# Near attention in a one-core encoder block: scaling the probabilities, or scaling the output

## The chip, the cores and the metric

The kernel runs on one core of one Trainium2 chip. The metric is the device time of one execution in microseconds, as the median of several executions. A profile is of one execution; its times are counted from the start of its span, and it names the engines PE (TensorE, the matmul engine, with PEld for its weight loads), DVE (VectorE), ACT (ScalarE), POOL (GpSimd) and SP (SyncE, which issues most transfers).

## What is computed

One layer of a bidirectional encoder on 1024 tokens of width 1024, in float32: layer norm, one combined projection, dilated attention in three groups of heads, a gated linear recurrence in both directions (HGRN2), gated merge, and a SwiGLU feed-forward part. The change lies in the attention, where each group of heads gives its own softmax output and the three are mixed with weights that come from their softmax denominators:

```python
def dilated_attention(aq, ak, av, slopes):
    ...
    for g, (window, dil) in enumerate(ATT_GROUPS):
        o, lse = dilated_group(aq[:, :, g], ak[:, :, g], av[:, :, g], window, dil, slopes[g])
        outs.append(o)
        lses.append(lse)
    w = jax.nn.softmax(jnp.stack(lses), axis=0)
    o = jnp.sum(w[..., None] * jnp.stack(outs), axis=0)
    return o.reshape(b, s, ATT_WIDTH).astype(aq.dtype)
```

Group 0 has a window of 128 tokens without dilation: this is the near attention. Groups 1 and 2, with dilations 4 and 16, are the far attention. For each token and head the kernel needs the exponentials of the near scores, their sum, and one factor that puts near and far on the same maximum and divides by the common sum.

## The kernel before, in words

All of the work runs in three phases. Phase 1, which holds the change, has a main stream and side units that are woven into it.

The stream (`stream`, lines 467 to 548) is the combined projection, in tiles of 128 columns. Four tiles at a time are computed by a seven-product scheme (`ORDER`); each product is four blocks of three matmuls (`mm3`, lines 253 to 257), because each operand is split into a rounded part and a rest. These matmuls write PSUM banks called `pj`, two for each group `g`. A product's weights are split by ScalarE (`w_hi`, line 205) and GpSimd (`w_lo`, line 209) three products ahead; sums of weight blocks are made at lines 488 to 493; a finished product is evacuated by VectorE or ScalarE (lines 401 to 430, and 511) before its bank can be written again.

Side units run in this order for each of four pairs of heads `j`: an HGRN head, another, the far attention (`att_far`), the near attention (`att_near`). Each unit is a generator. After each of its pieces it yields a number, which is how many products of the stream are issued before its next piece (`phase1`, lines 1124 to 1155). Within this, a scheduler at build time orders the instructions of each engine by its own estimate of their times, so an edit also shifts instructions around it. Each engine then runs its queue strictly in order. All side units share four PSUM banks (`ps_sd`) and nine SBUF slots of 128x1024 (`slot`), which are reused from unit to unit.

The near attention of one pair of heads (lines 780 to 892), as before:

- Scores: matmuls at line 811 for eight tiles of 128 queries and two heads; VectorE adds the bias and takes the row maximum (line 595); ScalarE takes the exponential with the row sum (line 827). Queries lie on the partitions, keys along the row. The exponentials lie in `P`, in slots 3, 4, 5 and 8.
- V is turned by TensorE (line 587) and copied by ScalarE (line 588).
- Factors (lines 833 to 842): `NM` is the common maximum, `W0` and `W12` become the factors of near and far for each query, 128x16 values each.
- Spread: GpSimd copies `W12`, each value 64 times, into `RB` (line 845, slot 1).
- Scaling: VectorE multiplies each row of each tile of `P` by `W0` (line 849): 18 instructions, fourteen of 128x256 and four of 64x128.
- Turn: TensorE transposes `P` tile by tile (line 863), VectorE and ScalarE copy the result back into `P` (lines 612 and 610).
- `RB` is transposed (line 870) into two banks `RL`, so that the factor of each query stands along the row.
- Output: matmuls of V and the turned `P` (line 883) into two banks `O`.
- Join: `OL`, the far output in slot 7, is multiplied by `RL` (line 888), `O` is added (line 890), and `OL` is stored (line 891).

Three of the four near units are followed by an HGRN head. It fetches into slots 1, 0 and 3, writes `qd` into slot 2 and, into slot 7, `fb` (line 937). Its scans and reciprocals are on VectorE (lines 953, 964, 967), its keys are finished by GpSimd (lines 961 and 965) and transposed by TensorE (line 982).

Of the kernel before, what the change touches and what calls it, by code (L numbers as in the profile page):

```python
# [14 lines left out]
OP = mybir.AluOpType  # L15
# [7 lines left out]
HALF = 512  # L23
# [56 lines left out]
class Block:  # L80
# [699 lines left out]
    def att_near(self, j, pre):  # L780


        nc, ident, HD, d = self.nc, self.ident, self.HD, self.at_d[j]
        OL, N12, L12 = self.far
# [6 lines left out]
        def rows(tt, hd):  # L791

            w = P[tt // 2][:, hd, tt % 2, :]
            if tt:
                return ((slice(0, 128), w),)
            return (slice(64, 128), w[64:128, 128:256]), (slice(0, 64), w[0:64, 0:128])
# [36 lines left out]
        NM, W0, W12 = (self.att_small(n) for n in ("NM", "W0", "W12"))  # L833
# [7 lines left out]
        for w in (W0, W12):  # L841
            nc.vector.tensor_mul(w, w, L0)

        RB = self.slot(1, "rb", (8, 2, 64))
        nc.gpsimd.tensor_copy(RB, W12.rearrange("p a t -> p t a")[:, :, :, None].to_broadcast([128, 8, 2, 64]))
        for tt in range(8):
            for hd in range(2):
                for p, z in rows(tt, hd):
                    nc.vector.tensor_scalar(z, z, W0[p, hd, tt:tt + 1], None, op0=OP.mult)  # L849
        yield 2  # L850

        kw = dict(skip_group_check=True)
# [4 lines left out]
        for b in range(4):  # L857
            for hd in range(2):
                ps = self.ps_sd()
# [4 lines left out]
                self.copied(hd, P[b][:, hd].rearrange("p t c -> p (t c)"), ps)  # L864
            if b % 2:
                yield b
        RL = [self.ps_sd(), self.ps_sd()]
        for tt in range(8):
            c = 128 * (tt % 4)
            nc.tensor.transpose(RL[tt // 4][:, c:c + 128], RB[:, tt].rearrange("p a d -> p (a d)"), ident)  # L870
        O = [self.ps_sd(), self.ps_sd()]
        todo = []
        for kt in range(8):
            c = 128 * (kt % 4)

            todo.append((kt, O[kt // 4], c + (64 if kt == 0 else 0), c + 128, kt, 192 if kt == 0 else 128))
            t = kt + 1
# [9 lines left out]
        for b, src, dst in cols:  # L887
            nc.vector.tensor_mul(OL[:, dst], OL[:, dst], RL[b][:, src])
        for b, src, dst in cols:
            nc.vector.tensor_add(OL[:, dst], OL[:, dst], O[b][:, src])  # L890
        nc.scalar.dma_start(self.att_d[j], OL)
        yield -1

# [843 lines left out]
```

## Time and profile before

| what | value |
|---|---|
| three executions | 2123.66, 2134.19, 2137.27 us; median 2134.19 |
| the profiled execution | 2131.49 us, its span 2129.7 us |
| mean granted clock of TensorE | 0.987 of full speed |
| near attention, pair 0 to 3: scaling from about | 360, 616, 868 and 1133 us |
| line 849: instructions, shortest, median, longest | 72: 278, 340 and 1268 ns |
| lines 888 and 890: instructions, median | 12 each: 617 and 610 ns |
| TensorE waits for line 849 | 8.6 us in 8 waits |

A row of the timeline has the start, the length, engine, line, operation, result<-operands, shapes and a count; what stands in brackets is the idle time of the engine before it and what ended that. Matmuls are pipelined, so the length of one is longer than the distance to the next. A row of the stretches has the length, the busy time of each engine (with its instructions), the granted clock, the share of the transfer engines and their GB/s. In a row of waits stand the waiting engine and line, what it waited for, the total in us, how often, and the longest.

### The profile page before, as it was taken

Reading aid. Unit: us, or ns where it says so; the run is one execution under the profiler, and the core shown is the slowest. Engines: PE = TensorE matmul, PEld = TensorE weight load, DVE = VectorE, ACT = ScalarE, POOL = GpSimd, SP = SyncE. Lnnn points to the kernel's source line nnn. Section 1 sums busy time; section 2 is a strip of 40 time slices with the busy share of each in tenths; the row PEclk is TensorE's granted clock in tenths of the full one; section 3 lists DMA queues with packets and bytes.
Section 4 is the critical chain, followed back from the end, with each engine's and each line's share of the span. In section 5 each row is a group of like instructions: output and inputs, shape, how many; then the busy total and the mean of one; then the engine's idle time right before and its main releaser. Section 6 shows DMA issues by size and latency. Waiting matters only on the chain.

```text
span 2129.7 us, 30900 instructions
## 1 busy us (share of the span) xinstructions
PE 2029.0 (95%) x10941; PEld 1674.6 (79%) x10941; DVE 1392.7 (65%) x2228; ACT 919.7 (43%) x1864; POOL 1077.5 (51%) x882
## 2 busy tenths in 40 slices
PE   4799999999999999999999899999999999999998
PEld 3678787788878788887888688878788888887876
DVE  7667746777459753788536712337867677767778
ACT  6544455434544435543355432135433333343542
POOL 3466653567536664465644754443656566630012
PEclk9899999999999999999999999999999999999999
DMA  5342442435424343333444755244434344348423
GB/s 202 109 133 95 147 155 73 144 118 167 130 92 141 135 146 125 124 129 109 146 130 142 283 188 164 89 139 139 154 109 153 129 144 134 117 160 291 158 89 124
DMA packets 273885, 301.10 MB, mean 141 GB/s; under 512 B 14081, under 2 KB 205378, under 8 KB 273730
## 3 DMA queue, kind: packets, MB, share of 16 engines
q1 hardware_dynamic: 266272, 273.73, 39.7%
q10 hardware_dynamic: 7458, 25.40, 3.0%
q8 instruction: 86, 1.41, 0.3%
q14 instruction: 69, 0.57, 0.1%
HBM read 200.25 MB, written 98.83 MB: 140 GB/s over the span
## 4 chain that ended last, share of the span: by engine, by line
PE 77%; DVE 12%; issue 5%; POOL 3%; DMA 2%; ACT 2%; SPq 0%; ACTq 0%; DVEq 0%; POOLq 0%
PE pj L255 17%; PE pj L256 17%; PE pj L257 16%; PE sd L256 6%; PE sd L255 6%; PE sd L257 6%; PE sd L1049 2%; POOL w_lo L209 1%; DVE qd L964 1%; DVE qd L967 1%; PE sd L998 1%; DVE p L849 1%; PE sd L863 1%; DVE fb L953 1%; ACT p L827 1%
## 5 line engine op out<-in xcount | busy, mean ns | idle before, releaser
L209 POOL TENSOR_TENSOR w_lo<-wa,w_hi 128x512 fp32r<-128x512 f32 x276 | 377.4, 1374 | 297.9 <-ACT w_hi L205 274.0
L205 ACT CAST w_hi<-wa 128x512 fp32r<-128x512 f32 x276 | 170.4, 619 | 245.8 <-PE pj L256 159.5
L209 POOL TENSOR_TENSOR w_lo<-wsum,w_hi 128x512 fp32r<-128x512 f32 x88 | 129.0, 1474 | 113.0 <-PE sd L257 60.4
L200 POOL TENSOR_TENSOR mv<-mv,mhalf 128x1 f32<-128x1 f32 x24 | 15.5, 647 | 228.6 <-DVE mv L199 225.5
L209 POOL TENSOR_TENSOR w_lo<-f_raw,w_hi 128x512 fp32r<-128x512 f32 x66 | 102.1, 1555 | 55.4 <-ACT w_hi L205 54.2
L255 PE MATMUL pj<-xt1hi,w_hi 128*128 128x512 f32 x260 | 103.9, 400 | 16.3 <-ACT xt1hi L205 10.7
L205 ACT CAST w_hi<-wsum 128x512 fp32r<-128x512 f32 x88 | 54.7, 621 | 124.6 <-PE sd L256 114.4
L255 PE MATMUL pj<-xb22hi,w_hi 128*128 128x512 f32 x260 | 102.6, 394 | 1.1 <-ACT wkeep L511 1.1
L256 PE MATMUL pj<-xt1lo,w_hi 128*128 128x512 f32 x260 | 102.3, 393 | 0.0
L257 PE MATMUL pj<-xt1hi,w_lo 128*128 128x512 f32 x260 | 102.0, 392 | 0.0
L256 PE MATMUL pj<-xb22lo,w_hi 128*128 128x512 f32 x260 | 101.5, 390 | 0.0
L257 PE MATMUL pj<-xb22hi,w_lo 128*128 128x512 f32 x260 | 101.3, 390 | 0.0
L209 POOL TENSOR_TENSOR w_lo<-ws,w_hi 128x512 fp32r<-128x512 f32 x46 | 63.0, 1373 | 69.2 <-ACT w_hi L205 63.3
L205 ACT CAST gwsum<-a_raw 128x512 fp32r<-128x512 f32 (+1 forms) x78 | 47.8, 616 | 102.9 <-PE pj L256 48.0
L511 ACT COPY wkeep<-pj 128x512 f32<-128x512 f32 x138 | 80.1, 582 | 22.1 <-DVE evh L430 10.1
L403 DVE TENSOR_TENSOR evh<-wkeep,pj 128x512 f32<-128x512 f32 x66 | 57.5, 879 | 48.5 <-PE pj L257 35.2
L209 DVE TENSOR_TENSOR gwkeep<-a_raw,gwsum 128x512 fp32r<-128x512 f32 (+1 forms) x78 | 57.7, 739 | 43.1 <-ACT gwsum L205 40.2
L489 POOL TENSOR_TENSOR wa<-wa,wa 128x512 f32<-128x512 f32 x46 | 67.6, 1480 | 35.6 <-DVE ws L488 27.6
L414 DVE TENSOR_TENSOR evh<-wkeep,pj 128x512 f32<-128x512 f32 x48 | 32.6, 681 | 80.7 <-PE pj L257 65.5
L255 PE MATMUL pj<-xt4hi,w_hi 128*128 128x512 f32 x192 | 77.8, 406 | 5.6 <-DVE evh L403 5.6
L257 PE MATMUL pj<-xt2hi,w_lo 128*128 128x512 f32 x192 | 76.1, 397 | 4.9 <-POOL w_lo L209 4.9
L255 PE MATMUL pj<-xb11hi,w_hi 128*128 128x512 f32 x192 | 77.3, 404 | 2.6 <-DVE evh L414 1.4
(406 smaller groups left out, 6587.1 us busy)
## 6 DMA issues: line engine op xcount, KB each, us to landing
wa<-in_w_in_dram SPq DMA_DIRECT2D x184, 256.0 KB, 3.1
f_raw<-in_w_ffn_in_dram SPq DMA_DIRECT2D x44, 512.0 KB, 4.2
a_raw<-gd SPq DMA_DIRECT2D x30, 512.0 KB, 3.5
gd<-fc SPq DMA_DIRECT2D x44, 256.0 KB, 2.0
gd<-fs SPq DMA_DIRECT2D x33, 256.0 KB, 2.1
tg<-evh SPq DMA_DIRECT2D x32, 256.0 KB, 3.5
tg<-tg SPq DMA_DIRECT2D x16, 512.0 KB, 3.7
y<-ahs SPq DMA_DIRECT2D x16, 512.0 KB, 5.5
```

Source lines behind the costliest of these rows:

```text
L205: nc.scalar.copy(hi, src)
L209: ins = e.tensor_sub(lo, src, hi.bitcast(F32))
L255: nc.tensor.matmul(ps, whi, xhi, start=first, stop=False, **kw)
L256: nc.tensor.matmul(ps, whi, xlo, start=False, stop=False, **kw)
L257: nc.tensor.matmul(ps, wlo, xhi, start=False, stop=last, **kw)
L403: self.left(nc.vector.tensor_tensor(o, self.order_src(add, g, kind), s, OP.add))
L414: self.left(nc.vector.tensor_add(t, add, ps))
L489: nc.gpsimd.tensor_sub(a["a21"], a["a11"], a["a21"])
L511: nc.scalar.copy(t, ps)
L827: nc.scalar.activation(z, z, AF.Exp, bias=N0[p, hd, tt:tt + 1], scale=QSCALE, accum_out=L0[p, hd, tt:tt + 1])
L849: nc.vector.tensor_scalar(z, z, W0[p, hd, tt:tt + 1], None, op0=OP.mult)
L1049: nc.tensor.matmul(po[:, jj, :], l, r, start=(n == 0), stop=(n == len(terms) - 1))
```

## The change

The probabilities are transposed as the exponentials leave them, without the factor. `W0` is spread by GpSimd into a second tile in the same way as `W12`, in slot 2, which held the keys of the near attention. That tile is transposed ahead of the other by eight more matmuls, and ScalarE copies the result into an SBUF tile `near`, also in slot 2. After the output matmuls, `near` is multiplied by the near output, and the product is added to the scaled far output. The 18 multiplications of line 849 are gone; in their place stand three of the shape of line 888. In the built order, the output matmuls stand 18 stream matmuls behind the spread's transposes, where before they followed them directly.

```diff
-        RB = self.slot(1, "rb", (8, 2, 64))
-        nc.gpsimd.tensor_copy(RB, W12.rearrange("p a t -> p t a")[:, :, :, None].to_broadcast([128, 8, 2, 64]))
-        for tt in range(8):
-            for hd in range(2):
-                for p, z in rows(tt, hd):
-                    nc.vector.tensor_scalar(z, z, W0[p, hd, tt:tt + 1], None, op0=OP.mult)
+        RB = [self.slot(1 + i, f"rb{i}", (8, 2, 64)) for i in range(2)]
+        for r, w in zip(RB, (W12, W0)):
+            nc.gpsimd.tensor_copy(r, w.rearrange("p a t -> p t a")[:, :, :, None].to_broadcast([128, 8, 2, 64]))
         yield 2
...
-        RL = [self.ps_sd(), self.ps_sd()]
-        for tt in range(8):
-            c = 128 * (tt % 4)
-            nc.tensor.transpose(RL[tt // 4][:, c:c + 128], RB[:, tt].rearrange("p a d -> p (a d)"), ident)
+        def spread(r):
+            out = [self.ps_sd(), self.ps_sd()]
+            for tt in range(8):
+                c = 128 * (tt % 4)
+                nc.tensor.transpose(out[tt // 4][:, c:c + 128], r[:, tt].rearrange("p a d -> p (a d)"), ident)
+            return out
+
+        near = self.slot(2, "near")
+        for b, ps in enumerate(spread(RB[1])):
+            nc.scalar.copy(near[:, HALF * b:HALF * (b + 1)], ps)
+        RL = spread(RB[0])
         O = [self.ps_sd(), self.ps_sd()]
...
         for b, src, dst in cols:
-            nc.vector.tensor_add(OL[:, dst], OL[:, dst], O[b][:, src])
+            z = slice(HALF * b + src.start, HALF * b + src.stop)
+            nc.vector.tensor_mul(near[:, z], near[:, z], O[b][:, src])
+            nc.vector.tensor_add(OL[:, dst], OL[:, dst], near[:, z])
         nc.scalar.dma_start(self.att_d[j], OL)
```

## The prediction

> **What bounds the kernel now.** I read the page first (shares of the span), then the chain that ended last, then who TensorE waits for, and last the four near-attention stages themselves, stretch by stretch and instruction by instruction.
>
> ```profile
> span 2129.7 us, 30900 instructions
> PE 2029.0 (95%) x10941; PEld 1674.6 (79%) x10941; DVE 1392.7 (65%) x2228; ACT 919.7 (43%) x1864; POOL 1077.5 (51%) x882
> PE   4799999999999999999999899999999999999998
> PEclk9899999999999999999999999999999999999999
> PE 77%; DVE 12%; issue 5%; POOL 3%; DMA 2%; ACT 2%; SPq 0%; ACTq 0%; DVEq 0%; POOLq 0%
> ```
>
> TensorE is busy for 2029.0 of 2129.7 us. An edit is worth what it does to TensorE: idle time taken away, matmuls added, or time at a lower granted clock. The other engines count only where TensorE waits for them. Of its 100 us of idle time, this is what the near attention owns (view of TensorE's waits):
>
> ```profile
> PE sd L863 <- DVE p L849: 8.6, 8, 2.0
> PE pj L255 <- DVE evh L403: 9.3, 4, 3.4
> ```
>
> The first line is the target: eight waits, two in each of the four near stages, in which the transposes of the probabilities (L863) stand behind VectorE's scaling (L849). The stage of head pair 0:
>
> ```profile
> 352.58 1.03 PE L587 MATMUL sd<-tabs_sb,v 128*128 128x128 f32 x8
> 357.10 0.39 PE L256 MATMUL pj<-xb21lo,w_hi 128*128 128x512 f32 x1
> 358.17 1.05 ACT L588 COPY v<-sd 128x512 f32<-128x512 f32 x2
> 359.82 0.39 PE L256 MATMUL pj<-xb21lo,w_hi 128*128 128x512 f32 x1
> 360.32 7.56 DVE L849 TENSOR_SCALAR p<-p,W 64x128 f32<-64x128 f32 x18
> 360.36 1.04 POOL L845 COPY rb<-W 128x1024 f32<-128x1024 f32 x1 [0.98 <-DVE W L842]
> 361.35 1.26 POOL L209 TENSOR_TENSOR w_lo<-wa,w_hi 128x512 fp32r<-128x512 f32 x1
> 362.75 0.65 PE L863 MATMUL sd<-tabs_sb,p 128*128 128x128 f32 x2 [1.86 <-DVE p L849]
> 364.26 3.30 PE L863 MATMUL sd<-tabs_sb,p 128*128 128x128 f32 x14 [0.87 <-DVE p L849]
> ```
>
> The stream's matmuls follow each other every 0.227 us (12 of them, 357.10 to 359.82). VectorE gets the factor W0 only at 360.3 and needs 7.56 us for 18 multiplications; TensorE stops twice, for 1.86 and 0.87 us. The four stages by stretch (us, then busy time of TensorE, its weight load, VectorE, ScalarE, GpSimd, then granted clock, DMA share, GB/s):
>
> ```profile
> 360.00:370.00 10.00, 7.27 (x27) 5.76 (x27) 9.88 (x24) 2.23 (x6) 3.48 (x3) 0.66 0.00 1
> 616.00:624.00 8.00, 6.09 (x33) 4.39 (x32) 7.94 (x19) 1.60 (x4) 3.19 (x3) 1.00 0.09 33
> 868.00:878.00 10.00, 7.99 (x36) 6.56 (x36) 9.84 (x23) 3.16 (x7) 3.13 (x3) 0.83 0.19 54
> 1134.00:1142.00 8.00, 6.01 (x34) 4.85 (x34) 7.95 (x19) 1.34 (x3) 3.61 (x3) 1.00 0.33 96
> ```
>
> Idle: 2.73 + 1.91 + 2.01 + 1.99 = 8.6 us, the sum of the waits above. In the first and third stage the granted clock falls as well: 7.27 busy us x (1 - 0.66) = 2.5 and 7.99 x (1 - 0.83) = 1.4, together 3.9 us of slow running.
>
> **The change, part by part.**
>
> *Removed: 72 scalings on VectorE (18 a stage).* The first transposes now need only the exponentials of row tiles 0 to 3 and PSUM. In the order of instructions as built, they stand 24 stream matmuls behind the transposes of V (L587) in every stage, where before there were 24 to 32. In stage 0, V's transposes end at about 353.4, so TensorE comes at 353.4 + 24 x 0.227 = 358.8. Of the four "sd" banks two are free by then and two wait for ScalarE's copies of V, which end at 358.7 and 359.2; the eight transposes ahead of that need take 0.9 us. So the wait goes: 8.6 us, and with it, if the dip is the stall's doing, 3.9 us of clock. What is late next is nothing on TensorE's own queue: the row factors are needed only 38 to 48 stream matmuls later (9 to 11 us), for the spread's transposes.
>
> *Added on TensorE: 8 more transposes a stage, 32 in all.* The same operation, by its line (minimum, median, maximum ns) and sixteen in one run:
>
> ```profile
> L863 PE MATMUL sd<-tabs_sb,p x128: 270/273/475, 362.7 to 1145.1; 128*128 128x128 f32 x128
> 878.40 1.91 PE L863 MATMUL sd<-tabs_sb,p 128*128 128x128 f32 x16
> 379.99 1.35 DVE L888 TENSOR_TENSOR ol<-ol,sd 128x448 f32<-128x448 f32 x3 [3.96 <-PE sd L870]
> 385.79 1.32 DVE L890 TENSOR_TENSOR ol<-ol,sd 128x512 f32<-128x512 f32 x3
> 377.18 0.58 ACT L511 COPY wkeep<-pj 128x512 f32<-128x512 f32 x1
> ```
>
> (1.91 - 0.27) / 15 = 0.109 us each, 0.273 being the median length of one, and TensorE has no gap to put them in: 32 x 0.109 = +3.5 us. The value is from the same operation, so I take it with no range to speak of.
>
> *Added on GpSimd: a second spread copy, 1.04 us a stage.* Both copies stand ahead of the next w_lo subtraction. In stage 0 that w_lo then ends near 363.7 instead of 362.6. GpSimd works about a product (12 matmuls, 2.7 us) ahead, and in the new order 16 transposes lie in between, so TensorE asks for it only near 368. Taken as 0; with the cover gone it would be 4 x 1.04 = 4.2 us.
>
> *Added on ScalarE: two copies of 128x512 from PSUM a stage*, 2 x 0.58 = 1.2 us by the copy above. The output matmuls (L883) stand 18 stream matmuls (4.1 us) behind the spread, because they reuse the copies' two banks; 4.1 covers 1.2 and the casts that may be ahead. Behind the copies queue the w_hi casts, again a product ahead. Taken as 0; uncovered 4.8 us.
>
> *Changed on VectorE at the end of a stage.* Three multiplications of `near` by the output in PSUM are new, as L888: 1.35 us. The three additions now read two SBUF tensors. The nearest rows are two such additions, one beside a running GpSimd:
>
> ```profile
> 353.11 1.75 DVE L490 TENSOR_TENSOR wa<-ws,wa 128x512 f32<-128x512 f32 x1
> 355.46 0.68 DVE L488 TENSOR_TENSOR ws<-wa,wa 128x512 f32<-128x512 f32 x1
> ```
>
> So the additions take about 1.4 (2 x 0.68) to 3.5 us (2 x 1.75) for 1.32 before. VectorE gains 7.6 us a stage and loses 1.4 to 3.5. It delays only the store of OL. No DMA is added; the store (ScalarE's queue) and the fetches into the slots move with their stage. The slot of `rb` frees for the next unit's first fetch behind the last spread transpose, as before.
>
> *What waits for the later store.* The next HGRN unit writes `fb` into OL's slot:
>
> ```profile
> 393.17 0.12 POOL L940 MEMSET fb<- 128x8 f32 x1 [3.62 <-DMA att<-ol]
> 394.35 1.63 DVE L953 TENSOR_TENSOR_SCAN fb<-fb,d 128x528 f32<-128x528 f32 x1
> 400.62 3.33 DVE L967 RECIPROCAL qd<-fb 128x256 f32<-128x256 f32 x2
> 401.88 2.48 POOL L965 TENSOR_TENSOR t<-t,qd 128x512 f32<-128x512 f32 x2
> 403.88 0.62 DVE L403 TENSOR_TENSOR evh<-wkeep,pj 128x512 f32<-128x512 f32 x1
> 404.64 0.77 PE L255 MATMUL pj<-xt4hi,w_hi 128*128 128x512 f32 x1 [3.39 <-DVE evh L403]
> 412.55 1.04 PE L982 MATMUL sd<-tabs_sb,t 128*128 128x128 f32 x8
> ```
>
> From OL's end (387.1) to the first direction's keys (half of L965, 403.1) are 16.0 us. In the new order the key transposes (L982) come 77, 90 and 91 stream matmuls and 8 transposes behind the output matmuls, that is 18.5, 21.4 and 21.7 us. The chain needs 1.35 + (1.4 to 3.5) + 16.0 = 18.8 to 20.9 us. So it is late by 0.3 to 2.4 us in the first and covered in the other two. I take +1.0, since part of the 16.0 is reciprocals that the new order puts behind evacuations.
>
> The sum: -8.6 - 3.9 + 3.5 + 1.0 = **-8.0 us**. The profiled execution took 2131.5 us (span 2129.7 and 1.8 around it), so 2123.5 by its own time; it lies 2.7 us under the median of the three runs, 2134.2, and the forecast for a median is 2134.2 - 8.0 = **2126 us**.
>
> [...] Stage 0 stood still for 1.86 and 0.87 us and the clock fell; stage 3 stood still for 1.99 us and it did not. By these rows the dip follows a stall sometimes, and taking the stalls away gives back 3.9 us. [...]
>
> **The rivals.**
>
> *The clock does not come back (2130 us).* The dips come from when a stall falls, not from these stalls alone; another stall collects them. For it: stages 1 and 3 show 1.00 after stalls of the same size. Against it: both dips begin inside the stall. Then -8.6 + 3.5 + 1.0 = -4.1.
>
> *More goes than the scaling (2118 us).* At 404.64 TensorE waits 3.39 us for an evacuation (L403) queued on VectorE behind scans and reciprocals (394.4 to 403.9, 9.5 us). The new order has an evacuation ahead of two scans, and no more than four reciprocals (6.6 us) between evacuations; a bank may stay full for three products, 3 x 2.7 = 8.2 us. So this stall may vanish. With its dip (row below: 10 - 7.36 = 2.6 idle inside the stretch, 7.36 x 0.34 = 2.5 of clock) it is 3.4 + 2.5 = 5.9: -8.0 - 5.9 = -13.9, or 2120; with a little of the last stalls, 2118.
>
> *It ends slower: the next unit meets the stream at a worse place (2146 us).* The HGRN work starts about 4 us later against the stream (18 matmuls), and its reciprocals of 3.3 us a pair may hold an evacuation beyond 8.2 us. One such stall costs 5.9 us as at 404; the same at the end of the phase, where ordering is rearranged too:
>
> ```profile
> 402.00:412.00 10.00, 7.36 (x20) 5.93 (x21) 10.00 (x11) 3.70 (x7) 8.91 (x8) 0.66 0.42 131
> 1180.00:1222.00 42.00, 34.96 (x147) 27.52 (x146) 31.30 (x23) 18.29 (x32) 34.70 (x19) 0.97 0.85 298
> ```
>
> Two new stalls (11.8) more than eat the 8.0; beyond 1.4 such stalls it is slower. Three or four of them (three units and the end of the phase), some 20 us, give -8.0 + 20 = +12, 2146. For it: the last stretch already loses 7.0 us idle. Against it: VectorE has some 5 us less to do in each stage.
>
> *The change doesn't do what it says (2138 us):* the transposes wait as long for ScalarE's exponentials or copies of V, so that only the 3.5 us remain. Against it: those end at 359.2, 1.1 us before the scaling even starts.
>
> **How the numbers follow.** Forecast 2126: 0.42. Clock stays: 0.2. More goes: 0.18. Worse place: 0.15. No effect: 0.05. Executions of the kernel before spread over 13.6 us (2123.7 to 2137.3), which widens every case. The 80% range reaches from the lower case less half that spread, 2118 - 5 = 2113, to 2141, into the slower case: **2113 to 2141**; the likeliest case alone, with its unknowns (0 to 2.4 at the keys, 3.9 of clock), 2121 to 2131. About 1%, 21 us, is what a measurement of this kernel can tell from no change. Below 2113 needs nearly all stalls of the phase gone: 0.06. Above 2155 needs five new stalls: 0.05. Within: 0.89.
>
> **What would show it.** Right: no wait of L863 for VectorE; clock 1.00 through the four stages; 64 spread transposes at 0.109 us; the casts and w_lo with no new wait of TensorE in these stages; VectorE some 20 us less busy. Wrong: TensorE waiting at the output matmuls for the copies into `near`, at w_lo behind the two spread copies, at L982 for `t`, or at an evacuation behind reciprocals, with a lower clock there.

## The result and the profile after

| | median us | runs | lowest to highest |
|---|---|---|---|
| before | 2131.94 | 6 | 2123.66 to 2137.27 |
| changed | 2112.49 | 6 | 2111.09 to 2116.44 |

The ratio is 0.9923 with a 95% interval of 0.9905 to 0.994: 19.5 us less, where the prediction said 8.0 less. By the bound of 1% it is no change; by its interval it is a small gain, and a bigger one than forecast. The two profiled executions differ by 20.4 us in span. The page of the changed kernel:

```profile
span 2109.3 us, 30917 instructions
PE 2022.3 (96%) x10973; PEld 1673.1 (79%) x10973; DVE 1373.2 (65%) x2168; ACT 925.0 (44%) x1872; POOL 1087.2 (52%) x886
PEclk9899999999999999999999999999999999999999
PE 78%; DVE 10%; issue 5%; POOL 3%; DMA 2%; ACT 1%; SPq 0%; DVEq 0%; ACTq 0%; POOLq 0%
```

TensorE is idle for 2109.3 - 2022.3 = 87.0 us, 13.7 less than before, and busy for 6.7 us less although it has 32 transposes more. VectorE is 19.5 us less busy ("some 20" was forecast). The waits of TensorE for the side units' work:

```profile
PE sd L1032 <- DVE hR L1015: 7.3, 4, 3.5
PE pj L257 <- POOL w_lo L209: 5.3, 6, 1.8
PE pj L255 <- DVE evh L403: 4.1, 3, 3.1
```

And the same two rows of the kernel before that the prediction did not show (L1026 and L1009 are L1032 and L1015 of the changed kernel):

```profile
PE pj L257 <- POOL w_lo L209: 6.6, 4, 2.9
PE sd L1026 <- DVE hR L1009: 2.9, 2, 2.1
```

The wait for the scaling is gone and nothing waits in its place. The evacuations (L403) cost 5.2 us less; the states of the HGRN head (`hR`) cost 4.4 us more. The four near stages by stretch, and the instructions of the first, in the changed kernel:

```profile
357.00:367.00 10.00, 10.00 (x62) 8.74 (x61) 7.70 (x17) 7.46 (x16) 7.70 (x7) 1.00 0.08 29
612.00:622.00 10.00, 10.00 (x56) 8.44 (x55) 4.82 (x6) 4.30 (x9) 8.04 (x6) 1.00 0.08 29
868.00:878.00 10.00, 10.00 (x54) 8.53 (x53) 4.88 (x9) 4.09 (x8) 5.92 (x5) 1.00 0.39 135
1126.00:1136.00 10.00, 10.00 (x54) 8.53 (x53) 5.12 (x7) 4.94 (x8) 3.87 (x3) 1.00 0.45 143
```

```profile
358.63 1.91 PE L860 MATMUL sd<-tabs_sb,p 128*128 128x128 f32 x16
359.97 2.03 POOL L846 COPY rb<-W 128x1024 f32<-128x1024 f32 x2 [0.89 <-DVE W L842]
360.50 1.28 DVE L612 COPY p<-sd 128x512 f32<-128x512 f32 x2
364.03 1.91 PE L860 MATMUL sd<-tabs_sb,p 128*128 128x128 f32 x16
374.13 1.07 ACT L873 COPY near<-sd 128x512 f32<-128x512 f32 x2
382.49 1.35 DVE L895 TENSOR_TENSOR near<-near,sd 128x512 f32<-128x512 f32 x3 [1.86 <-PE sd L887]
383.76 2.45 DVE L896 TENSOR_TENSOR ol<-ol,near 128x512 f32<-128x512 f32 x3
```

TensorE is busy without a gap and at full clock in all four. The transposes start at 358.63 (the prediction computed 358.8) with no wait in brackets, before W0 is spread, and VectorE copies their banks at once.

To see where the 20.4 us came from, count the stream's matmuls (L255 to L257): there are 7596 in both kernels, in the same order, so the time between two of the same number can be compared, stretch by stretch. Change against the kernel before, in us, one profiled execution each:

| stretch | changed | e1 | e3 | e8 | e9 | e10 | e11 |
|---|---|---|---|---|---|---|---|
| the four near stages | -11.7 | -15.3 | +5.3 | +3.9 | -11.8 | -13.4 | -12.4 |
| HGRN head behind pair 0 | -3.8 | -3.3 | -3.8 | -4.0 | -4.1 | -1.9 | -4.5 |
| HGRN heads behind pairs 1, 2 | +0.2 | -0.6 | -1.3 | -0.9 | +0.5 | -1.5 | +1.0 |
| rest of phase 1 behind pair 3 | -2.7 | +2.1 | -3.2 | -3.5 | -3.7 | +1.3 | +0.9 |
| phases 2 and 3 | -2.2 | -0.2 | +0.4 | +0.2 | -1.7 | -2.8 | +1.6 |

(e1 to e11 are the experiments below. What is left, the start, the far stages and the last part of the heads behind pair 1, is between -0.5 and +1.8. Phases 2 and 3 are the same code in all of them, so differences of 2 to 3 us there are not the change. Part of them is clock: the kernel before runs four stretches of 3.4 us at half clock there, the changed kernel, e9 and e10 three; the granted clock is 0.5 in them, so one costs up to half its length, 1.7 us.)

### The profile page after: what moved, and what is told of

Read it like the earlier page. It is cut to its first block, busy times and chain, and to the rows that moved or that the text cites. A ratio compares the mean times of both kernels' runs of the same rounds, so it can differ in the third digit from the quotient of the medians.

```text
span 2109.3 us, 30917 instructions
## 1 busy us (share of the span) xinstructions
PE 2022.3 (96%) x10973; PEld 1673.1 (79%) x10973; DVE 1373.2 (65%) x2168; ACT 925.0 (44%) x1872; POOL 1087.2 (52%) x886
## 4 chain that ended last, share of the span: by engine, by line
PE 78%; DVE 10%; issue 5%; POOL 3%; DMA 2%; ACT 1%; SPq 0%; DVEq 0%; ACTq 0%; POOLq 0%
PE pj L255 17%; PE pj L256 17%; PE pj L257 17%; PE sd L255 6%; PE sd L256 6%; PE sd L257 6%; PE sd L1055 2%; POOL w_lo L209 2%; DVE qd L970 1%; DVE hR L1016 1%; DVE qd L973 1%; PE sd L811 1%; PE sd L860 1%; PE sd L887 1%; DVE hR L1015 1%
## 5 line engine op out<-in xcount | busy, mean ns | idle before, releaser
L209 POOL TENSOR_TENSOR w_lo<-wa,w_hi 128x512 fp32r<-128x512 f32 x276 | 382.2, 1392 | 301.0 <-ACT w_hi L205 271.0
L209 POOL TENSOR_TENSOR w_lo<-wsum,w_hi 128x512 fp32r<-128x512 f32 x88 | 128.7, 1472 | 112.7 <-PE sd L257 60.7
L209 POOL TENSOR_TENSOR w_lo<-f_raw,w_hi 128x512 fp32r<-128x512 f32 x66 | 102.0, 1554 | 55.8 <-ACT w_hi L205 54.6
L255 PE MATMUL pj<-xt1hi,w_hi 128*128 128x512 f32 x260 | 104.7, 403 | 17.4 <-ACT xt1hi L205 10.7
L257 PE MATMUL pj<-xt1hi,w_lo 128*128 128x512 f32 x260 | 102.6, 395 | 1.0 <-POOL w_lo L209 1.0
L255 PE MATMUL pj<-xb22hi,w_hi 128*128 128x512 f32 x260 | 102.5, 394 | 0.0
L257 PE MATMUL pj<-xb22hi,w_lo 128*128 128x512 f32 x260 | 101.6, 391 | 0.0
L209 POOL TENSOR_TENSOR w_lo<-ws,w_hi 128x512 fp32r<-128x512 f32 x46 | 64.5, 1406 | 60.9 <-ACT w_hi L205 58.8
L403 DVE TENSOR_TENSOR evh<-wkeep,pj 128x512 f32<-128x512 f32 x66 | 57.6, 879 | 50.2 <-PE pj L257 35.4
L209 DVE TENSOR_TENSOR gwkeep<-a_raw,gwsum 128x512 fp32r<-128x512 f32 (+1 forms) x78 | 57.8, 742 | 40.5 <-ACT gwsum L205 37.6
L255 PE MATMUL pj<-xt2hi,w_hi 128*128 128x512 f32 x192 | 77.9, 407 | 2.6 <-ACT xt2hi L205 1.8
L255 PE MATMUL pj<-xb11hi,w_hi 128*128 128x512 f32 x192 | 77.4, 404 | 2.7 <-DVE evh L414 1.5
L257 PE MATMUL pj<-xt2hi,w_lo 128*128 128x512 f32 x192 | 76.0, 396 | 2.4 <-POOL w_lo L209 2.4
```

The source lines that it names most:

```text
L209: ins = e.tensor_sub(lo, src, hi.bitcast(F32))
L255: nc.tensor.matmul(ps, whi, xhi, start=first, stop=False, **kw)
L257: nc.tensor.matmul(ps, wlo, xhi, start=False, stop=last, **kw)
L403: self.left(nc.vector.tensor_tensor(o, self.order_src(add, g, kind), s, OP.add))
```

## The experiments

Four theories appear. The *stop theory* is the prediction's: the transposes need the scaled values, and without this dependence the stop is gone. The *load theory*: VectorE had too many hours of work in phase 1, and any work on it costs. The *order theory*: the gain lies in the units behind the near stages, which the built order places anew. The *block theory*, formed after the third run: what costs is work that stands in VectorE's queue ahead of the copies that free the transposes' banks, whether its result is used or not. In this table the third column is TensorE's wait at the transposes of `P`, for whatever engine. The ratio is to executions of the kernel before that were made together with the run; their medians lie between 2127.73 and 2131.94 us.

| run | median us | wait at the transposes, us | ratio, 95% interval |
|---|---|---|---|
| changed | 2112.49 | 0 | 0.9923, 0.9905 to 0.994 |
| e1 no scaling | 2111.6 | 0 | 0.992, 0.9895 to 0.9945 |
| e2 scaling and spread | 2131.94 | 11.3 | 1.0012, 0.9998 to 1.0025 |
| e3 unread work, old place | 2131.66 | 11.4 | 1.0017, 1.0004 to 1.0031 |
| e4 transposes later | 2119.92 | 8.0 | 0.9956, 0.9943 to 0.9969 |
| e5 scaling in two halves | 2115.82 | 4.2 | 0.9944, 0.9927 to 0.9961 |
| e6 states elsewhere | 2114.23 | 0 | 0.9932, 0.9914 to 0.995 |
| e7 half of e3's work | 2119.52 | 5.4 | 0.9958, 0.9944 to 0.9972 |
| e8 meant behind the copies | 2130.02 | 11.4 | 1.0009, 0.9997 to 1.002 |
| e9 truly behind the copies | 2112.84 | 0 | 0.9929, 0.9912 to 0.9946 |
| e10 scaling on two engines | 2117.3 | 1.0 | 0.9945, 0.9928 to 0.9962 |
| e11 scaling on ScalarE | 2118.93 | 0.4 | 0.9953, 0.9939 to 0.9968 |
| e12 as e10, output later | 2113.66 | 0.9 | 0.9917, 0.9889 to 0.9946 |

**e1: the scaling away, nothing in its place** (kernel before; the near part stays without its factor).

```diff
-        for tt in range(8):
-            for hd in range(2):
-                for p, z in rows(tt, hd):
-                    nc.vector.tensor_scalar(z, z, W0[p, hd, tt:tt + 1], None, op0=OP.mult)
```

> The kernel before without the 18 multiplications of each near stage and with nothing in their place: the near probabilities keep no factor, so the near part of the attention is left unnormalised. Stop theory (the gain is TensorE's stop at the transposes behind VectorE, and the clock that falls with it): TensorE no longer waits there, the four near stages together give back about 8.6 of idle, 1.3 hidden in the modelled ends of the last matmul before each stop and up to 3.9 of clock, 12 to 14 us, some 3.5 more than the near stages of the changed kernel gave (11.7), since no transposes are added. Load theory (the gain is VectorE's lighter queue, wherever it lets evacuations through): the whole kernel is at least as fast as the changed one, 2105 to 2113, and the gain is spread over the HGRN units behind. Order theory (the gain is what the build-time order does to the units behind): the near stages as in the stop theory, but the total anywhere from 2112 to 2135.

2111.6 us. The whole gain comes from taking the scaling off; what the change adds is hardly seen in the total. The total alone would fit the load theory too (2105 to 2113), but that wanted the gain spread over the HGRN units, and 15.3 of the 16.9 us between the two profiles lie in the near stages. In the near stages e1 gains 15.3 and the changed kernel 11.7, so the additions cost 3.6 us there (3.5 forecast for the transposes alone). e1 also settles a point about the clock. The stall for L403 of the kernel before is still there in e1:

```profile
398.27 0.47 PE L255 MATMUL pj<-xt4hi,w_hi 128*128 128x512 f32 x1 [2.91 <-DVE evh L403]
390.00:405.00 15.00, 12.09 (x62) 10.03 (x61) 15.00 (x12) 5.90 (x12) 14.72 (x13) 1.00 0.41 123
```

Nearly the same stop, 2.91 us (3.39 before), but the granted clock stays at 1.00, where it fell to 0.77 over these 15 us in the kernel before:

```profile
397.00:412.00 15.00, 11.61 (x43) 9.30 (x43) 15.00 (x14) 4.94 (x9) 13.91 (x13) 0.77 0.34 105
```

So most of the 3.3 us that e1 gains in this head is clock; the last section has the two stops by windows of the clock.

**e2: the scaling put back into the changed kernel** (the near part is then scaled twice).

```diff
             nc.gpsimd.tensor_copy(r, w.rearrange("p a t -> p t a")[:, :, :, None].to_broadcast([128, 8, 2, 64]))
+        for tt in range(8):
+            for hd in range(2):
+                for p, z in rows(tt, hd):
+                    nc.vector.tensor_scalar(z, z, W0[p, hd, tt:tt + 1], None, op0=OP.mult)
         yield 2
```

> The changed kernel with the 18 multiplications put back as well, so the near part is scaled twice (by the square of its factor). Stop theory: TensorE stops again at the transposes, 8 us or more of idle there, and the 32 added transposes cost 3.5 us on top: 2133 to 2142. Load theory: VectorE has all of the old work and 1.4 to 3.5 us a stage more: slower than before, 2138 to 2148. Order theory: the units behind the near stages are ordered nearly as in the changed kernel, so their part of the gain, some 8 us, stays: 2122 to 2130.

2131.94 us, between the ranges of the order theory and the stop theory, and 2.9 us above the kernel before in the same session (2129.09): the gain is gone, and all that the change adds and reorders is not what brought it.

```profile
PE sd L864 <- DVE p L850: 11.3, 7, 2.7
```

**e3: 18 multiplications at the old place whose result nobody reads** (changed kernel; they work on the bias tiles, which are done with).

```diff
+        for n in range(18):
+            z = bias[n % 2][:, 0:128 if n < 4 else 256]
+            nc.vector.tensor_scalar(z, z, W0[:, n % 2, n % 8:n % 8 + 1], None, op0=OP.mult)
         yield 2
```

> The changed kernel with 18 multiplications of the old shapes on VectorE at the old place in its queue, but on a bias tile that nobody reads any more, so that the transposes don't wait for them. The result is the changed kernel's. Stop theory: no wait at the transposes' data; VectorE's copies of the turned probabilities and its evacuations are some 7 us late, which the stream's three products of 8.2 us nearly cover: near stages at least 8 us better than before, total 2113 to 2124. Load theory: VectorE is as full as before, so the gain is gone: 2128 to 2138. Order theory: as the changed kernel, 2108 to 2118, where the order behind is the same.

2131.66 us, the load theory's number. No transpose depends on these multiplications, and the gain is gone all the same; the stop theory is not enough, and neither is the order theory (2108 to 2118). TensorE's and VectorE's rows of pair 0:

```profile
359.14 1.91 PE L863 MATMUL sd<-tabs_sb,p 128*128 128x128 f32 x16
360.45 6.99 DVE L849 TENSOR_SCALAR bias<-bias,W 128x128 f32<-128x128 f32 x13
364.99 0.60 PE L863 MATMUL sd<-tabs_sb,p 128*128 128x128 f32 x4
368.48 0.68 DVE L612 COPY p<-sd 128x512 f32<-128x512 f32 x1
369.22 1.89 PE L863 MATMUL sd<-tabs_sb,p 128*128 128x128 f32 x12 [3.63 <-DVE p L612]
```

The first sixteen transposes run at once and fill the four banks. VectorE must copy two of these, but in its queue the block of multiplications stands first (360.45, for 6.99 us), and it did not take the copy ahead of it. The copy starts at 368.48, 8.0 us later than in the changed kernel (360.50), and the second sixteen transposes stop for 3.63 us until then. The stop has only moved from the operand to the banks.

**e4: the transposes two products later** (kernel before; `yield 4` for 2 ahead of them, `yield 1` for 3 behind).

```diff
-        yield 2
+        yield 4
...
-                yield b
+                yield 1
```

> The kernel before, same work, with two more products of the stream (5.4 us) issued between the scaling and the transposes of the probabilities, and two fewer behind the transposes. Stop theory: TensorE comes to the transposes when the scaling is nearly done, the stops shrink from 8.6 us to under 2, and without the added transposes the near stages give 10 to 13 us: total 2115 to 2125. Load theory: VectorE's queue is the same, so the time is that of before within 5 us: 2127 to 2137. Order theory: as the stop theory in the near stages, plus or minus 8 us in the units behind, which begin at another place of the stream.

2119.92 us, half of the gain, with VectorE's work untouched. That speaks against the load theory (2127 to 2137). The number is the stop theory's, but its stop did not shrink to under 2 us: 8.0 us remain, now at VectorE's copies (L612), 5.2 of them in one stop. In the built order the first transposes stand 14 to 19 stream matmuls later, where two products would be 24. The profiled execution is the slowest of ten (2126.47 us).

```profile
PE sd L863 <- DVE p L612: 8.0, 3, 5.2
PE pj L255 <- DVE evh L414: 6.6, 2, 5.4
```

**e5: the scaling in two halves, the transposes between** (kernel before).

```diff
+        scale(range(4))
-        yield 2
+        yield 3
...
-            if b % 2:
-                yield b
+            if b == 1:
+                scale(range(4, 8))
+                yield 2
+        yield 1
```

> The kernel before with the scaling cut in two: the row tiles 0 to 3 are scaled first, and three products of the stream are issued before their transposes; the tiles 4 to 7 are scaled behind the copies of the first transposes, with two products before theirs. Same instructions on every engine, none added. Block theory (what stops TensorE is that VectorE has 7.6 us in one piece, with the copies of the turned probabilities and the evacuations queued behind it): pieces of about 3.8 us lie beside two or three products (5.4 to 8.2 us), so the stops are nearly gone, and without 3.5 us of added transposes the near stages give 12 to 15 us: 2112 to 2120. Load theory (the amount of VectorE work decides): no gain, 2126 to 2134.

2115.82 us, most of the gain, with all 72 multiplications on VectorE: the block theory's number, but not by its means. In all four pairs the scheduler left the 18 multiplications ahead of the first copies (L612), in pair 0 in one row:

```profile
361.26 7.57 DVE L851 TENSOR_SCALAR p<-p,W 64x128 f32<-64x128 f32 x18
369.96 1.27 DVE L612 COPY p<-sd 128x512 f32<-128x512 f32 x2
```

What the edit did change is the transposes' place: the first sixteen stand 4 to 12 stream matmuls later than in the kernel before, the second 11 to 20. So e5 shows the worth of the later place; the halving was not tested.

**e6: the HGRN states one product earlier**, against the new wait for `hR` (changed kernel; two of the yields in `hgrn_side`).

```diff
         k0 = self.hgrn_keys(st, 0)
-        yield 3
+        yield 2
...
         S[1] = self.hgrn_states(st, 1, k1, vT)
-        yield 3
+        yield 4
```

> The changed kernel, and in every HGRN head the first states are issued two instead of three products behind their keys, and the scores four instead of three products behind the last states. TensorE's 7.3 us of waits of the scores for the states (hR) should fall under 3: a gain of 4 to 7 us with the slower clock behind such stops, 2105 to 2109. Order theory: the other instructions move too and the gain is anywhere between -8 and +8.

2114.23 us, and `hR` still waits 7.4 us: missed. But the edit hardly took effect. In the built order the scores stand behind the same stream matmuls as in the changed kernel in every head, and some states moved by 1 to 12. In the head with the long stop both stand where they stood, and the stop is 3.46 us (3.45 in the changed kernel). So this run says nothing on whether earlier states would help.

**e7: e3 with 9 multiplications.**

```diff
+        for n in range(9):
```

> The changed kernel with 9 instead of 18 multiplications on VectorE that nobody reads, at the old place. Block theory: 3.5 us in front of the copies is within what the stream's three products cover, so most of the gain stays: waits of the second transposes for VectorE's copies under 3 us (11.0 with 18), total 2113 to 2119. Load theory: half of the gain, 2120 to 2124.

2119.52 us with 5.4 us of waits at the transposes. The nine take 5.93 us in pair 0, not 3.5: the first four of a block, beside GpSimd, took 1.15 us each on average in e3 and e8 (last section). They cost 7 of the 19 us of gain; the time falls between the two theories' ranges, so by itself it tells little.

**e8 and e9: the unread work behind the copies** (changed kernel). e8 has e3's three lines just ahead of `near = ...`; e9 differs from e8 in one operand:

```diff
-            nc.vector.tensor_scalar(z, z, W0[:, n % 2, n % 8:n % 8 + 1], None, op0=OP.mult)
+            nc.vector.tensor_scalar(z, tile(7, 0)[:, 0:128 if n < 4 else 256], W0[:, n % 2, n % 8:n % 8 + 1], None, op0=OP.mult)
```

> The changed kernel with all 18 multiplications that nobody reads, but behind the copies of the turned probabilities in VectorE's queue, where the spread follows. Same work on VectorE as in the run with 18 at the old place. Block theory: no wait of the second transposes for the copies; only evacuations stand behind the block, and they have 8.2 us against 7: 2113 to 2121. Load theory: as with 18 at the old place, 2127 to 2136.

2130.02 us, by the number a win for the load theory. But the timeline of e8 shows that the edit did not do what was meant. Its inputs are ready as soon as W0 is, and the build-time scheduler put the work at the old place, ahead of the copies:

```profile
361.41 6.99 DVE L873 TENSOR_SCALAR bias<-bias,W 128x128 f32<-128x128 f32 x13
369.44 0.68 DVE L612 COPY p<-sd 128x512 f32<-128x512 f32 x1
370.18 1.93 PE L860 MATMUL sd<-tabs_sb,p 128*128 128x128 f32 x12 [3.64 <-DVE p L612]
```

So e8 only repeats e3. e9 takes the last copied block as its input, which holds the work behind the copies:

> The changed kernel with 18 unread multiplications whose input is the last transposed block, so that VectorE cannot take them before its four copies of that pair (in the run before this one their inputs were ready earlier, and they ran ahead of the copies all the same). Block theory (what costs is the work that stands in VectorE's queue between the scores and the copies of the transposed blocks): no wait of the transposes for VectorE's copies (11.0 us in 4 stops there), 2112 to 2121 us; the upper end, if the evacuations of the stream that stand behind the block in pairs 1 to 3 cost a stop each of up to 2 us. Load theory (VectorE as full as before costs what it cost before, wherever the work stands): 2127 to 2134 us, with stops of 8 to 11 us in total at some other place.

2112.84 us, the time of the changed kernel. Its rows of VectorE in pair 0, and its busy time:

```profile
360.26 1.28 DVE L612 COPY p<-sd 128x512 f32<-128x512 f32 x2
364.42 0.69 DVE L612 COPY p<-sd 128x512 f32<-128x512 f32 x1 [0.59 <-PE sd L860]
367.16 0.68 DVE L612 COPY p<-sd 128x512 f32<-128x512 f32 x1
367.88 5.66 DVE L873 TENSOR_SCALAR bias<-p,W 128x128 f32<-128x128 f32 x18
PE 2022.3 (96%) x10973; PEld 1673.0 (79%) x10973; DVE 1398.8 (66%) x2240; ACT 925.6 (44%) x1872; POOL 1093.7 (52%) x886
```

VectorE is 1398.8 us busy, more than in the kernel before (1392.7), and nothing is lost. This decides between the theories: not the hours of VectorE but the place of the block. (The block of e9 is also shorter, 7.1 us a pair against 9.6 in e8, but that is not the reason: e7's, with about 6 us, stops TensorE at the old place.) In the near stages e8 and e9 lie 15.7 us apart (+3.9 and -11.8).

**e10 and e11: the scaling on another engine** (kernel before; ScalarE takes the second head, as in the diff, or in e11 both).

```diff
-                    nc.vector.tensor_scalar(z, z, W0[p, hd, tt:tt + 1], None, op0=OP.mult)
+                    if hd:
+                        nc.scalar.activation(z, z, AF.Copy, scale=W0[p, hd, tt:tt + 1])
+                    else:
+                        nc.vector.tensor_scalar(z, z, W0[p, hd, tt:tt + 1], None, op0=OP.mult)
```

> The kernel before, with the scalings of the second head given to ScalarE (9 of 18 in each pair; ScalarE's timeline there shows 7.8 us without work, and its scaled copies of 128x128 take 0.40 us). No added transposes. Block theory: half a block on each of two engines, some 4.5 us instead of 9.5, so that TensorE stops at the first transposes for under 4 us in total, 2109 to 2118 us. Load theory, by half of VectorE's work: 2119 to 2125 us.

> The kernel before, with all 18 scalings of a pair given to ScalarE. VectorE is as empty as in the changed kernel, but the block of 18 x 0.4 to 0.5 = 7 to 9 us stands ahead of the transposes all the same, on another engine. Block theory: TensorE stops at the transposes for ScalarE, 5 to 11 us in total, 2118 to 2130 us. Load theory (VectorE's hours are what counts): no such stop, 2108 to 2114 us.

2117.3 and 2118.93 us. e10 came out as the block theory said, a stop of 1.0 us in all. e11's total fell into the block theory's range, but not for its reason: TensorE waits 0.4 us at the transposes, not 5 to 11.

```profile
360.00 2.08 ACT L849 ACTIVATE p<-p,W 64x128 f32<-64x128 f32 x5 [1.08 <-DVE W L842]
362.49 0.91 ACT L849 ACTIVATE p<-p,W 128x256 f32<-128x256 f32 x2
363.77 4.51 ACT L849 ACTIVATE p<-p,W 128x256 f32<-128x256 f32 x11
```

In its built order the transposes are spread between stream matmuls (in pairs 0 and 3 two to eight at a time, behind each scaled tile), and the stream covers the block. In the near stages e10 and e11 gain more than the changed kernel (13.4 and 12.4 against 11.7), since they add no transposes. They lose it in the rest of phase 1 (+1.3 and +0.9, against -2.7).

**e12: e10 with the output matmuls 12 stream matmuls behind the spread**, because the rest of phase 1 gained in the kernels whose output stands later.

```diff
+        yield 1
         O = [self.ps_sd(), self.ps_sd()]
```

> As the run with the scaling on two engines (2117.3 us), and in addition one yield between the spread's transposes and the output matmuls, so that these stand 12 stream matmuls behind the spread in every pair (18 in the changed kernel, 0 in the kernel before). No added transposes. In the kernels compared so far, the stretch from the last near attention to the end of phase 1 took 2.7 to 3.8 us less than before where the output stands later (changed kernel, and those with unread multiplications), and 0.9 to 2.1 us more where the scaling was taken off VectorE without that. If the place of the output is the cause, that stretch gets 3 to 5 us shorter than in the run with two engines and the time is 2111 to 2115 us, about the changed kernel's. If it is not, the stretch stays and the time is 2115 to 2120 us.

2113.66 us, the number forecast, but the stretch hardly shrank (+0.8 against the kernel before; +1.3 in e10). So the cause named in the expectation is not shown, and that the number came is luck. No kernel here is faster than the changed one beyond the intervals.

## Why the prediction was right, and where it was too small

- *The transposes no longer wait: right.* 8.6 us of idle time are gone, and the prediction's place for them (358.8) held to 0.2 us. The reason given was half of it: the operand. e3 shows that the stop comes back without the operand as long as VectorE's copies stand behind the block; e9 shows that 18 such multiplications behind the copies are free. (The eight waits were read as two in each stage; by the timeline they are 2, 3, 2 and 1. The sum is the same.)
- *The clock in these stages: right in sign, too small, and in part luck.* It is 1.00 in all four. In the kernel before, TensorE was busy for 2.55, 3.41 and 3.26 us at half clock in the first and the third stage, so about half of that, 4.6 us, was lost (an estimate from the granted 0.50; there the stream's matmuls follow each other every 0.427 us, 405.20 to 409.47, and at full clock every 0.227). The prediction had 3.9, because it took the mean clock over stretches that hold the idle time as well. That there were dips was a near thing: in the last section's count, windows in which TensorE was busy for less than 1.5 us were all followed by half clock and those with 1.7 us or more never, and 1.55 us, as in both stages, lies between, where either came.
- *The added transposes, +3.5: right.* 64 of them at (1.91 for sixteen) 0.109 us; e1 puts all additions at 3.6. The two spread copies on GpSimd (2.03 us), the copies into `near` (1.07 us) and the additions (2.45 us, between the bounds 1.4 and 3.5) made TensorE wait nowhere in these stages: from 350 to 390, 596 to 640, 850 to 892 and 1112 to 1155 us no row of TensorE has a wait in brackets.
- *The sum in the near stages: -9.0 forecast, -11.7 measured.* Taking the scaling away brought 15.3 where 8.6 + 3.9 = 12.5 were counted. A part is how idle time is counted: it begins at the modelled end of the last matmul, 0.39 us behind its start, while the next could have started after 0.227. Eight stops of 0.16 make 1.3. The clock makes another 0.7, as above. The other 0.8 us I can't assign.
- *What follows, +1.0: wrong, and this is the step that failed.* The prediction let only the key transposes be late and took everything else behind the near stages as unchanged. TensorE's waits for the keys stayed at 0.6 us at most. The head behind pair 0 became 3.8 us shorter: its stall for L403 and the half clock went, as the rival "more goes than the scaling" had it (2118 us, 0.18). About the part of the stream that lay at 397 to 412 us before is the first row below: TensorE is hardly idle and at full clock. That rival, not the likeliest case, is nearest to what happened. Its opposite is there as well, as the wait for `hR`, once with a dip as in the rival "worse place":

```profile
388.00:403.00 15.00, 14.82 (x74) 12.23 (x73) 15.00 (x13) 7.18 (x12) 12.64 (x13) 1.00 0.37 127
681.24 0.37 PE L1032 MATMUL sd<-qd,t 128*64 128x64 f32 x1 [3.45 <-DVE hR L1015]
675.00:690.00 15.00, 11.55 (x106) 9.59 (x105) 11.17 (x22) 7.41 (x18) 7.00 (x7) 0.77 0.39 113
```

- *The rest of phase 1, -2.7, and phases 2 and 3, -2.2,* had no term. The first is of the same sign in every kernel made from the changed one that stands in the table (-2.7 to -3.7) and so seems to belong to its order; why, stays open, since e12 did not bring it about. Clock is part of it: the kernel before and e9 run 3.4 us at half clock there, the changed kernel, e3 and e8 none, e10 and e11 twice that, e1 three times. But e9, with as much as before, gains most. The second is within what the same code shows from run to run.
- *The size.* 2112.49 lies 13.5 us under the forecast and 0.5 under the range's low end. Some 2 us of this are the reference: the three executions it was drawn on had their median at 2134.19, six have 2131.94. The low end was also worked out wrongly: half the spread of 13.6 is 6.8, not 5, and 2118 - 6.8 is 2111. The 0.89 stands for 2113 to 2155, not for the range given. And 1% is not the least that can be told: the interval here is 0.9905 to 0.994.

## What to carry over

VectorE, which frees the banks that TensorE writes, was a gate here: 18 multiplications a pair ahead of those copies in its queue stopped TensorE for 11.0 us in all even though nobody reads the result (e3), and 18 behind them were free (e9, 2112.84 against 2112.49 us). So before an operation is paid for with other instructions, look whether it can be put behind the copies, or the transposes later (e5), or the work on an engine that idles there (e10, e12): e12 and e5 come within 1 to 4 us of the changed kernel's median without one added transpose. And when an edit moves side work against the stream, price the stalls that follow as well as the one removed, and check in the built order that an experiment's edit landed where it was meant.

## What the runs showed of the hardware

**The clock went with TensorE's busy time in windows of 3.413 us.** In each of the fourteen traces all changes of the granted clock, between 1.0 and 0.5, lie whole multiples of 3.413 us apart, so they stand on a grid. Between 330 and 2060 us the traces hold 6979 such windows at full clock. In 78 of them TensorE was busy for less than 1.5 us (by the profile's modelled ends), and behind every one of these the next window ran at half clock. In 6884 it was busy for 1.7 us or more, and none of these was followed by half clock. Of the 17 between, 6 were. The traces of the two kernels alone hold 995 of them: 10 below 1.5 us, 981 at 1.7 or more, and 4 between (1.55 and 1.55 us with half clock behind them, 1.624 and 1.698 us without). They also hold 17 windows at half clock. Where TensorE was busy for 2.92 us or more in one of these, 12 times, the next was at full clock again; where it was busy for 2.56 us or less, 5 times, it was not.

So the dips go not with the length of a stop alone but with how much of it falls into one window. Two windows of the kernel before, at 1.55 and 0.87 us, were followed by half clock:

```profile
359.42:362.83 3.41, 1.55 (x8) 0.97 (x7) 3.23 (x8) 1.33 (x3) 2.47 (x3) 1.00 0.00 0
400.38:403.79 3.41, 0.87 (x8) 0.63 (x6) 3.41 (x3) 0.47 (x1) 3.41 (x4) 1.00 0.15 42
```

In e1 nearly the same stop for L403 lay across two windows, and the clock stayed:

```profile
393.80:397.21 3.41, 1.55 (x11) 1.15 (x10) 3.41 (x3) 0.62 (x1) 3.41 (x4) 1.00 0.09 21
397.21:400.62 3.41, 2.35 (x10) 1.99 (x11) 3.41 (x5) 1.59 (x3) 3.41 (x5) 1.00 0.78 192
```

The stop of 3.45 us for `hR` in the changed kernel fell mostly into one window (first row) and brought a dip; the one of 3.46 us in e6 was split (second and third row) and did not:

```profile
676.56:679.98 3.42, 1.23 (x30) 0.98 (x25) 2.97 (x8) 2.34 (x6) 1.27 (x1) 1.00 0.00 0
677.04:680.46 3.42, 1.75 (x46) 1.52 (x41) 2.87 (x8) 2.29 (x6) 1.27 (x1) 1.00 0.00 0
680.46:683.87 3.41, 1.62 (x35) 1.54 (x36) 3.34 (x7) 1.93 (x5) 1.51 (x2) 1.00 0.24 84
```

A dip lasts 3.4 or 6.8 us here, one window or two. In pair 0 of the kernel before one began at 362.83, right behind the stop of 1.86 us; the one of 0.87 us lies inside it. The grid lies otherwise in each trace: in the rows above a window begins about 1.0 (before), 1.3 (e1), 0.7 (changed) and 1.2 us (e6) behind a whole multiple of 3.413 us from the span's start. So by these rows the same stop can count in one execution and not in another. This is read from the traces; no run here moved a stop against the grid on purpose.

**The same multiplication took 0.43 or 1.15 us on average.** In e8 nearly all of the first four of each block ran beside GpSimd's spread copies or the weight splits (L209) behind them, in e9 most did not:

```profile
L873 DVE TENSOR_SCALAR bias<-bias,W 128x128 f32<-128x128 f32 x16 | 17.5, 1151 | 0.0
```

```profile
L873 DVE TENSOR_SCALAR bias<-p,W 128x128 f32<-128x128 f32 x16 | 6.0, 434 | 0.1
```

The slow ones end with GpSimd's instructions: each of the multiplications of over 0.6 us, 13 in the kernel before, 20 in e8 and 10 in e9, ends 0.08 or 0.15 us behind the end of a GpSimd instruction. In pair 0 of the kernel before, the second ends just behind the weight split of 361.35 to 362.61, and the fourth runs alone:

```profile
361.49 1.20 DVE L849 TENSOR_SCALAR p<-p,W 64x128 f32<-64x128 f32 x1
363.93 0.28 DVE L849 TENSOR_SCALAR p<-p,W 64x128 f32<-64x128 f32 x1
```

It goes the other way as well: beside the running block of e9 a weight split took 3.58 us, where the median of this shape is 1.29 (514 in the kernel before):

```profile
371.09 3.58 POOL L209 TENSOR_TENSOR w_lo<-wa,w_hi 128x512 fp32r<-128x512 f32 x1 [1.71 <-ACT w_hi L205]
```

It makes the old place of the scaling dearer: 13 of the sixteen small ones in the kernel before ran beside GpSimd too, and the longest of them took 1.27 us. What in the two engines brings it about, no run here shows.
